# Hybrid decoder step: the products of a weight unit ordered by output tile, and in the FFN blocks in sixteen orders by turns

## The chip, the cores and the metric

The kernel runs on one core of one Trainium2 chip. The page of the profile names the core's engines: PE multiplies matrices (PEld is its loading of the stationary operand), DVE and ACT work elementwise, POOL does a little elementwise work and issues DMAs, SP issues DMAs. The metric is the device time of one execution in microseconds; of several executions the median counts.

## The reference, cut to what matters

One layer works on 256 prompt tokens and 8 × 4 sample tokens, 288 columns in all, with a model width of 2048 and an FFN width of 5632.

```
x = x + 0.5 * rmsnorm(swiglu(rmsnorm(x, g0), ffn1_w_in, ffn1_w_out), g1)
x = x + rmsnorm(hybrid_mixer(rmsnorm(x, g2), mix_w_in, ..., mix_w_out), g3)
x = x + 0.5 * rmsnorm(swiglu(rmsnorm(x, g4), ffn2_w_in, ffn2_w_out), g5)

swiglu(x):        gate, up = split(x @ w_in, 2);  (silu(gate) * up) @ w_out
hybrid_mixer(h):  proj = h @ w_in                 # q, k, v, gates of two groups of heads
                  two recurrences S_t = diag(a_t) S_{t-1} + k_t^T v_t, o_t = q_t S_t
                  merged @ w_out
```

The outputs are y for the prompt and for the sample, and the recurrent states of both. All of it is float32.

## The kernel before, in words

The tokens are the columns of every product: a tile of activations is 128 features by 288 tokens. For accuracy each float32 operand is kept as a high and a low part, and a product of two operands is made as three matmuls into one PSUM tile. `mm3` records them, always in this order; this document calls them A, B and C.

- A (line 596): high weights by high activations
- B (line 597): high weights by low activations
- C (line 598): low weights by high activations

Weights come from memory in *units* of 128 × 1024 numbers, two activation tiles' worth (k = 2u and 2u + 1, called the two *halves* of the unit) by 512 output columns. `Weights.load` issues the DMA on SP, and `Weights.pieces` makes the high part on ACT (line 100) and the low part on DVE (line 101). Up to three raw units and four split ones are held; each engine's order is the order in which the program records the work, and `W.ahead` records further splits after each unit.

`block` (line 587) makes one block of 512 output columns: four PSUM tiles f = 0 to 3 of 128 columns, from all units. A block of the FFNs' input side (`gate` and `up`, eleven of each in each FFN) and each block of the mixer has 16 activation tiles, so eight units, of 4 × 2 × 3 = 24 matmuls each, 192 in all. A block of the FFNs' output side (`out`) has two units (48 matmuls), the last four in each FFN have four. In all units of a block but the last, the order before is by activation tile: for each half, for each f, the three matmuls A, B, C. The last unit, the *tail*, goes by output tile: for each f, both halves, A, B, C of each. After each f of the tail that tile is evacuated from PSUM (`evac`): in a gate block by DVE at line 676. There are five PSUM tiles for blocks, so a block's tiles f = 1, 2, 3 take the places of the block before's f = 0, 1, 2.

An FFN goes through chunks c = 0 to 10: gate c, up c, then the four out blocks of chunk c − 1. In the first blocks after a norm (`gate1_0`, `qk0`, `gate2_0`) the activation tiles become ready one after another while the block runs. In the mixer, `tick` records pieces of the recurrences between products, small matmuls among them, after each activation tile. In the mixer's last gate block, `tick_last` records the splits of the merged outputs (`split_y`), which overwrite the activation tiles that this block reads.

Of the kernel before, what the change touches and what calls it, by code (L numbers as in the profile page):

```python
# [16 lines left out]
P = 128  # L17
TP = 256
TS = 32
T = TP + TS  # L20
# [3 lines left out]
KT = D // P  # L24
# [14 lines left out]
class Weights:  # L39
# [91 lines left out]
def trunk_kernel(ctx, tc, x_prompt, x_sample, state_gla, state_hgrn, norm_gains, f1_in, f1_out, f2_in, f2_out,  # L131
# [3 lines left out]
    V, S, G, PE = nc.vector, nc.scalar, nc.gpsimd, nc.tensor  # L135
# [107 lines left out]
    FIRST = 2  # L243
# [339 lines left out]


    product = [None]

    def block(name, nk, rhs, evac, width=512, tick=None, tail=1, hold=False, most=99, fill=None, late=0):

        nf, per = width // P, 1024 // width
        nu = nk // per  # L590
        ps = [mmtile(f"{name}_{f}") for f in range(nf)]
        ws = [W.next() for _ in range(EARLY // per)] if fill else []

        def mm3(dst, w, f, k, parts, start, stop):
            a, c = k % per, slice(f * P, f * P + P)
            yield lambda: PE.matmul(dst, w[0][:, a, c], parts[0], start=start, stop=False)  # L596
            yield lambda: PE.matmul(dst, w[0][:, a, c], parts[1], start=False, stop=False)  # L597
            yield lambda: PE.matmul(dst, w[1][:, a, c], parts[0], start=False, stop=stop)  # L598

        def mm(w, f, k):  # L600
            if not fill or f or k >= EARLY:
                for ready in mm3(ps[f][:, 0:T], w, f, k, rhs(k), k == 0, k == nk - 1):
                    product[0] = ready().ins

        if fill:
            fill.products(lambda dst, k, parts, stop: mm3(dst, ws[k // per], 0, k, parts, k == 0, stop), ps[0][:, 0:T])
        for u in range(nu - tail):
            w = ws.pop(0) if ws else W.next()
            for k in range(u * per, (u + 1) * per):
                if fill and k < UPDATED:  # L610
# [38 lines left out]
    def ffn(tag, gcol, gnext, pn, before, fill=None):  # L649
# [3 lines left out]
        with ExitStack() as pools:  # L653
# [3 lines left out]
            def do_in(c):  # L657
                hh = fp.tile([P, 4, T], F32R, name=f"hh{tag}_{c}", tag="hh")
                hl = fp.tile([P, 4, T], F32R, name=f"hl{tag}_{c}", tag="hl")
                hid[c] = (hh, hl)  # L660
                gs = []

                def gate(g):
                    def run():
                        V.tensor_tensor(g, g, rt, op=ALU.mult)
                        act(g, g, AF.Silu)
                    return run

                def ev_gate(f, ps):
                    g = fp.tile([P, T], F32, name="g", tag="g", bufs=6)  # L670
                    gs.append(g)
                    if c == 0:
                        W.behind = S.activation(g, ps, AF.Copy).ins
                        pn.late.append(gate(g))
                    else:
                        V.tensor_tensor(g, ps, rt, op=ALU.mult)
                        act(g, g, AF.Silu)

                def ev_up(f, ps):
                    u = fp.tile([P, T], F32, name="u", tag="u", bufs=3)  # L680
                    V.tensor_tensor(u, ps, rt, op=ALU.mult)  # L681
                    V.tensor_tensor(u, u, gs[f], op=ALU.mult)
                    S.activation(hh[:, f, :], u, AF.Copy)
                    V.tensor_tensor(hl[:, f, :], u, hh[:, f, :].bitcast(F32), op=ALU.subtract)

                if c == 0:
                    block(f"gate{tag}_0", KT, xrhs, ev_gate, tick=pn.tick0, most=1 if final else 0, fill=fill,
                          late=0 if final else FIRST)
                    before.close()
                    if not final:  # L690
                        border.append(Border(mixer_start, hg1, gnext, 5, 2))
                else:
                    block(f"gate{tag}_{c}", KT, xrhs, ev_gate)
                if final and c == 0:
                    last_pool()
                block(f"up{tag}_{c}", KT, xrhs, ev_up, tick=pn.tick1 if c == 0 else None)

            lasts, zs, blocks = [], [], []

# [167 lines left out]
    def mixer(pn, border):  # L867
        with ExitStack() as mx:
# [667 lines left out]
            for g in range(2):  # L1536
                d = group_tiles(f"g{g}")
                block(f"qk{g}", KT, xrhs, ev_gla(d, g == 0), tick=tick if g else pn.tick0, most=99 if g else 1,
                      fill=None if g else border.fill)
                if g == 0:  # L1540
                    scan_pool()
                if g == 0:
# [55 lines left out]
            def split_y(t):  # L1598
                S.activation(xh[t], y[t], AF.Copy)
                V.tensor_tensor(xl[t], y[t], xh[t].bitcast(F32), op=ALU.subtract)  # L1600
# [6 lines left out]
                    tick(k)  # L1607

            def tick_last(k):
                if k < 12:  # L1610
                    split_y(k)

            for n in range(4):
                block(f"gate{n}", KT, xrhs, ev_gate(n), tick=(tick, tick, tick_silu, tick_last)[n])
# [79 lines left out]
```

## Time and profile before

| | us |
|---|---|
| three runs | 2226.94, 2227.61, 2229.22 |
| median | 2227.61 |
| profiled execution | 2226.28 |
| its span, first to last instruction | 2224.5 |
| PE busy | 2212.8 |
| DVE busy | 1386.7 |
| ACT busy | 1020.1 |
| POOL busy | 180.2 |

Engines work at the same time, so the busy times don't add up to the span. PE's matmuls overlap each other in the records (a row of 0.29 us is followed by the next after some 0.13 us); what a matmul costs in a row of them is therefore read from the distance of starts, not from the duration.

### The profile page before, as it was taken

How to read it: one execution, taken by the hardware profiler on the slowest of the kernel's cores; microseconds unless marked ns; L12 is line 12 of the kernel's file. 1: busy time of each engine (PE TensorE's matmuls, PEld its weight loads, DVE VectorE, ACT ScalarE, POOL GpSimd, SP SyncE). 2: the span in 40 equal slices, each digit the busy share in tenths (PEclk: the TensorE clock that was granted, in tenths of full speed). 3: DMA queues.
4: the chain of work that ended last, by engine and by line, in shares of the span. 5: the costliest groups of instructions: out<-in, count | busy, mean ns of one | idle time of the engine just before them, and what ended most of it. 6: DMA issues, size and time to landing. Idle time of an engine off the chain costs nothing. (4 is left out here: it accounts for less than half of the span.)

```text
span 2224.5 us, 43196 instructions
## 1 busy us (share of the span) xinstructions
PE 2212.8 (99%) x17820; PEld 2197.9 (99%) x17820; DVE 1386.7 (62%) x2254; ACT 1020.1 (46%) x1535; POOL 180.2 (8%) x327
## 2 busy tenths in 40 slices
PE   9999999999999999999999999999999999999998
PEld 9999999999999999999999999999999999999998
DVE  7645546554555568888888755844555466556646
ACT  6453333333334345655676654543333333333344
POOL 2000000000000001233210000000000020122005
PEclk9999999999999999999999999999999999999999
DMA  7555555555555554667566564555555565566555
GB/s 224 173 166 167 170 167 166 170 165 168 171 164 181 177 165 139 193 204 214 171 188 179 174 185 133 171 168 165 170 167 165 170 176 168 179 178 176 171 162 159
DMA packets 227334, 384.87 MB, mean 173 GB/s; under 512 B 21362, under 2 KB 60864, under 8 KB 227136
## 3 DMA queue, kind: packets, MB, share of 16 engines
q1 hardware_dynamic: 213776, 364.89, 54.8%
q0 software_dynamic: 10992, 16.77, 2.9%
q8 instruction: 140, 2.29, 0.4%
q10 hardware_dynamic: 2368, 0.44, 0.1%
q14 instruction: 58, 0.48, 0.1%
HBM read 363.75 MB, written 11.80 MB: 169 GB/s over the span
## 5 line engine op out<-in xcount | busy, mean ns | idle before, releaser
L101 DVE TENSOR_TENSOR wh<-raw,wh 128x1024 fp32r<-128x1024 f32 (+1 forms) x676 | 821.8, 1217 | 619.0 <-ACT wh L100 617.5
L100 ACT ACTIVATE wh<-raw 128x1024 fp32r<-128x1024 f32 (+1 forms) x676 | 711.0, 1053 | 961.0 <-PE gate L598 301.8
L596 PE MATMUL gate<-xh,wh 128*128 128x288 f32 x1660 | 485.5, 294 | 0.0
L598 PE MATMUL gate<-xh,wh 128*128 128x288 f32 x1660 | 484.8, 293 | 0.0
L597 PE MATMUL gate<-xl,wh 128*128 128x288 f32 x1660 | 484.7, 294 | 0.0
L597 PE MATMUL out<-hl,wh 128*128 128x288 f32 x1408 | 416.2, 296 | 0.0
L597 PE MATMUL up<-xl,wh 128*128 128x288 f32 x1408 | 413.9, 294 | 0.0
L598 PE MATMUL up<-xh,wh 128*128 128x288 f32 x1408 | 412.8, 293 | 0.0
L598 PE MATMUL out<-hh,wh 128*128 128x288 f32 x1408 | 412.1, 293 | 0.0
L596 PE MATMUL up<-xh,wh 128*128 128x288 f32 x1408 | 411.8, 293 | 0.0
L596 PE MATMUL out<-hh,wh 128*128 128x288 f32 x1408 | 411.5, 292 | 0.0
L596 PEld LDWEIGHTS gate<-xh,wh 128*128 128x128 f32 x1660 | 311.2, 188 | 0.8 <-DVE u L681 0.4
L598 PEld LDWEIGHTS gate<-xh,wh 128*128 128x128 f32 x1660 | 311.1, 188 | 0.2 <-DVE wh L101 0.2
L597 PEld LDWEIGHTS gate<-xl,wh 128*128 128x128 f32 x1660 | 310.5, 188 | 0.5
L596 PEld LDWEIGHTS out<-hh,wh 128*128 128x128 f32 x1408 | 264.9, 188 | 0.0
L596 PEld LDWEIGHTS up<-xh,wh 128*128 128x128 f32 x1408 | 264.4, 188 | 0.0
L597 PEld LDWEIGHTS out<-hl,wh 128*128 128x128 f32 x1408 | 264.3, 188 | 0.0
L598 PEld LDWEIGHTS out<-hh,wh 128*128 128x128 f32 x1408 | 264.3, 188 | 0.0
L597 PEld LDWEIGHTS up<-xl,wh 128*128 128x128 f32 x1408 | 264.2, 188 | 0.0
L598 PEld LDWEIGHTS up<-xh,wh 128*128 128x128 f32 x1408 | 264.2, 188 | 0.0
L770 DVE TENSOR_TENSOR y<-out,y 128x288 f32<-128x288 f32 x287 | 120.7, 452 | 85.2 <-PE out L598 84.1
L727 POOL DMA_DIRECT2D xT<-b x64 | 37.2, 588 | 764.8 <-PE gate L598 571.8
(410 smaller groups left out, 2550.3 us busy)
## 6 DMA issues: line engine op xcount, KB each, us to landing
raw<-in_ffn_w_in_dram SPq DMA_DIRECT2D x350, 512.0 KB, 3.6
raw<-in_ffn_w_out_dram SPq DMA_DIRECT2D x176, 512.0 KB, 3.6
raw<-in_mix_w_in_dram SPq DMA_DIRECT2D x64, 512.0 KB, 4.1
raw<-in_mix_w_in_dram SPq DMA_DIRECT2D x96, 256.0 KB, 3.2
raw<-in_mix_w_out_dram SPq DMA_DIRECT2D x32, 512.0 KB, 3.8
out_dram<-s POOLq DMA_DIRECT2D x32, 256.0 KB, 2.9
s<-in_state_gla_dram SPq DMA_DIRECT2D x16, 256.0 KB, 4.9
s<-in_state_hgrn_dram SPq DMA_DIRECT2D x16, 256.0 KB, 5.2
```

The source lines that it names most:

```text
L100: i1 = self.nc.scalar.activation(h[:, a, c], raw[:, a, c], AF.Copy).ins
L101: i2 = self.nc.vector.tensor_tensor(l[:, a, c], raw[:, a, c], h[:, a, c].bitcast(F32), op=ALU.subtract).ins
L596: yield lambda: PE.matmul(dst, w[0][:, a, c], parts[0], start=start, stop=False)
L597: yield lambda: PE.matmul(dst, w[0][:, a, c], parts[1], start=False, stop=False)
L598: yield lambda: PE.matmul(dst, w[1][:, a, c], parts[0], start=False, stop=stop)
L727: queues[n % len(queues)].dma_start(dst[q * TS:(q + 1) * TS, 4 * g:4 * g + 4, :, cols].rearrange("p k t c -> p (k t) c"), b32[rows, q])
L770: V.tensor_tensor(y[k], ps, y[k], op=ALU.add)
```

## The change

Three things change, all in the order in which `block` records its matmuls. No matmul, transfer or elementwise instruction is added or removed.

1. By default a unit's matmuls now go as the tail's do, by output tile: for each f, both halves, A, B, C of each. `tick` is called after f = 1 and after f = 3, so as often as before and after as many matmuls. This holds for all out blocks, for `up1_0` and `up2_0`, for all blocks of the mixer but `qk0`, and for the `mo` blocks (the mixer's output projection).
2. `gate1_0`, `gate2_0` and `qk0` keep the old order (`byk=True`).
3. The 40 other gate and up blocks (c = 1 to 10 in both FFNs) take, for all units but the tail, one of sixteen orders from the table `ways`: gate takes number (20·tag + 2c) mod 16 and up the next, where tag is 1 or 2.

With `split_y` called two activation tiles later, no tile is overwritten that a later f of the same unit still reads.

The sixteen orders differ in what changes from one matmul to the next. By how often two successive matmuls belong to different halves of the unit, and so to different activation tiles k, they fall into four groups:

| Half changes | Orders | Blocks |
|---|---|---|
| after every 3 matmuls, as in the tail | 0, 1, 3, 6, 14, 15 | 13 |
| after every 6 | 12, 13 | 6 |
| after every 12, as in the order before | 8, 9, 10 | 9 |
| after every one (2, 5, 11) or after 4 of 6 (4, 7) | 2, 4, 5, 7, 11 | 12 |

Order 15 also takes the output tiles from f = 3 down to 0. The diff, with two of the sixteen rows for f, half a and product j in full:

```diff
     product = [None]
-
-    def block(name, nk, rhs, evac, width=512, tick=None, tail=1, hold=False, most=99, fill=None, late=0):
+    by = lambda fs, kj: [(f, a, j) for f in fs for a, j in kj]
+    A, B, C = 0, 1, 2
+    ways = [
+        by(range(4), [(0, A), (0, B), (0, C), (1, A), (1, B), (1, C)]),
...
+        by(range(4), [(0, A), (1, A), (0, B), (1, B), (0, C), (1, C)]),
...
+        [(f, a, j) for a in range(2) for f in range(4) for j in range(3)],
...
+        [(f, a, j) for f in range(3, -1, -1) for a in range(2) for j in range(3)],
+    ]
+
+    def block(name, nk, rhs, evac, width=512, tick=None, tail=1, hold=False, most=99, fill=None, late=0, byk=False, way=None):
...
         for u in range(nu - tail):
             w = ws.pop(0) if ws else W.next()
-            for k in range(u * per, (u + 1) * per):
+            if way is not None:
+                for f, a, j in ways[way]:
+                    k = u * per + a
+                    q, r = ((0, 0), (0, 1), (1, 0))[j]
+                    begin = u == 0 and (f, a, j) == next(e for e in ways[way] if e[0] == f)
+                    product[0] = PE.matmul(ps[f][:, 0:T], w[q][:, a, f * P:f * P + P], rhs(k)[r],
+                                           start=begin, stop=False).ins
+            elif not byk:
+                for f in range(nf):
+                    for k in range(u * per, (u + 1) * per):
+                        mm(w, f, k)
+                    if tick is not None and f % 2:
+                        tick(u * per + f // 2)
+            for k in range(u * per, (u + 1) * per) if byk else ():
...
-                    block(f"gate{tag}_{c}", KT, xrhs, ev_gate)
+                    block(f"gate{tag}_{c}", KT, xrhs, ev_gate, way=(20 * tag + 2 * c) % 16)
...
-                block(f"up{tag}_{c}", KT, xrhs, ev_up, tick=pn.tick1 if c == 0 else None)
+                block(f"up{tag}_{c}", KT, xrhs, ev_up, tick=pn.tick1 if c == 0 else None,
+                      way=(20 * tag + 2 * c + 1) % 16 if c else None)
...
             def tick_last(k):
-                if k < 12:
-                    split_y(k)
+                if 2 <= k < 14:
+                    split_y(k - 2)
```

What stands in PE's row at three places, in the names that the program gives: `mo2_1` is tile f = 1 of the third `mo` block, `xh1` and `xl1` are the high and the low part of activation tile 1, `wh` is a split unit. Lines 596 to 598 of the kernel before are lines 616 to 618 now; the sixteen orders are recorded at line 634.

PE at the start of block `mo2` (an out block reads likewise, with the FFN's inner activations in place of `xh` and `xl`), before:

```order
L596 MATMUL mo2_0_15486<-xh0_114,wh392_15320 128x288
L597 MATMUL mo2_0_15486<-xl0_130,wh392_15320 128x288
L598 MATMUL mo2_0_15486<-xh0_114,wh392_15320 128x288
L596 MATMUL mo2_1_15487<-xh0_114,wh392_15320 128x288
L597 MATMUL mo2_1_15487<-xl0_130,wh392_15320 128x288
L598 MATMUL mo2_1_15487<-xh0_114,wh392_15320 128x288
L596 MATMUL mo2_2_15488<-xh0_114,wh392_15320 128x288
```

PE at the same place now:

```order
L616 MATMUL mo2_0_15486<-xh0_114,wh392_15320 128x288
L617 MATMUL mo2_0_15486<-xl0_130,wh392_15320 128x288
L618 MATMUL mo2_0_15486<-xh0_114,wh392_15320 128x288
L616 MATMUL mo2_0_15486<-xh1_115,wh392_15320 128x288
L617 MATMUL mo2_0_15486<-xl1_131,wh392_15320 128x288
L618 MATMUL mo2_0_15486<-xh1_115,wh392_15320 128x288
L616 MATMUL mo2_1_15487<-xh0_114,wh392_15320 128x288
```

Six matmuls now go to one output tile in succession, three of each half, where three did.

PE in the first unit of `gate1_7`, which takes order 2, before:

```order
L598 MATMUL gate1_7_0_5579<-xh0_114,wh160_5473 128x288
L596 MATMUL gate1_7_1_5580<-xh0_114,wh160_5473 128x288
L597 MATMUL gate1_7_1_5580<-xl0_130,wh160_5473 128x288
L598 MATMUL gate1_7_1_5580<-xh0_114,wh160_5473 128x288
L596 MATMUL gate1_7_2_5581<-xh0_114,wh160_5473 128x288
```

PE in the same unit now, from its third matmul on:

```order
L634 MATMUL gate1_7_0_5579<-xl0_130,wh160_5473 128x288
L634 MATMUL gate1_7_0_5579<-xl1_131,wh160_5473 128x288
L634 MATMUL gate1_7_0_5579<-xh0_114,wh160_5473 128x288
L634 MATMUL gate1_7_0_5579<-xh1_115,wh160_5473 128x288
L634 MATMUL gate1_7_1_5580<-xh0_114,wh160_5473 128x288
```

Here the half changes with every matmul.

PE at the border of `gate1_5` and `up1_5`, which takes order 15, before:

```order
L596 MATMUL gate1_5_3_4042<-xh15_129,wh119_4154 128x288
L597 MATMUL gate1_5_3_4042<-xl15_145,wh119_4154 128x288
L598 MATMUL gate1_5_3_4042<-xh15_129,wh119_4154 128x288
L596 MATMUL up1_5_0_4287<-xh0_114,wh120_4183 128x288
L597 MATMUL up1_5_0_4287<-xl0_130,wh120_4183 128x288
```

PE at the same border now:

```order
L616 MATMUL gate1_5_3_4042<-xh15_129,wh119_4154 128x288
L617 MATMUL gate1_5_3_4042<-xl15_145,wh119_4154 128x288
L618 MATMUL gate1_5_3_4042<-xh15_129,wh119_4154 128x288
L634 MATMUL up1_5_3_4290<-xh0_114,wh120_4183 128x288
L634 MATMUL up1_5_3_4290<-xl0_130,wh120_4183 128x288
```

Tile f = 3, which takes the PSUM place of `gate1_5`'s f = 2, is now written first where it was written tenth. On DVE, ACT, POOL and SP the order of the instructions is the one before, but for the mixer's last gate block, where each weight split now stands one `split_y` earlier among the splits.

More of the change, by code (lines that the diff above doesn't have):

```diff
@@ L585, in trunk_kernel @@
     product = [None]
-    def block(name, nk, rhs, evac, width=512, tick=None, tail=1, hold=False, most=99, fill=None, late=0):
+    by = lambda fs, kj: [(f, a, j) for f in fs for a, j in kj]
+    A, B, C = 0, 1, 2
+    ways = [
+        by(range(4), [(0, A), (0, B), (0, C), (1, A), (1, B), (1, C)]),
+        by(range(4), [(0, A), (0, C), (0, B), (1, A), (1, C), (1, B)]),
+        by(range(4), [(0, A), (1, A), (0, B), (1, B), (0, C), (1, C)]),
+        by(range(4), [(0, A), (0, B), (0, C), (1, C), (1, B), (1, A)]),
+        by(range(4), [(0, B), (0, A), (1, A), (1, B), (0, C), (1, C)]),
+        by(range(4), [(0, A), (1, A), (0, C), (1, C), (0, B), (1, B)]),
+        by(range(4), [(0, C), (0, A), (0, B), (1, B), (1, A), (1, C)]),
+        by(range(4), [(0, A), (0, B), (1, A), (1, B), (0, C), (1, C)]),
+        [(f, a, j) for a in range(2) for f in range(4) for j in range(3)],
+        [(f, a, j) for a in range(2) for j in range(3) for f in range(4)],
+        [(f, a, j) for a in range(2) for f, j in [(f, j) for f in range(4) for j in (A, C)] + [(f, B) for f in range(4)]],
+        [(f, a, j) for j in range(3) for f in range(4) for a in range(2)],
+        [(f, a, j) for g in range(2) for a in range(2) for j in range(3) for f in (2 * g, 2 * g + 1)],
+        [(f, a if f % 2 else 1 - a, j) for f in range(4) for a in range(2) for j in range(3)],
+        [(f, a, j if f % 2 else 2 - j) for f in range(4) for a in range(2) for j in range(3)],
+        [(f, a, j) for f in range(3, -1, -1) for a in range(2) for j in range(3)],
+    ]
+    def block(name, nk, rhs, evac, width=512, tick=None, tail=1, hold=False, most=99, fill=None, late=0, byk=False, way=None):
         nf, per = width // P, 1024 // width
@@ L687, in do_in @@
                     block(f"gate{tag}_0", KT, xrhs, ev_gate, tick=pn.tick0, most=1 if final else 0, fill=fill,
-                          late=0 if final else FIRST)
+                          late=0 if final else FIRST, byk=True)
                     before.close()
@@ L1538, in mixer @@
                 block(f"qk{g}", KT, xrhs, ev_gla(d, g == 0), tick=tick if g else pn.tick0, most=99 if g else 1,
-                      fill=None if g else border.fill)
+                      fill=None if g else border.fill, byk=not g)
                 if g == 0:
```

## The prediction

> **What bounds the kernel now.** I read the page's busy times first, then PE's waits, then the busy time of single blocks, and last the matmuls in order of time.
>
> ```profile
> span 2224.5 us, 43196 instructions
> PE 2212.8 (99%) x17820; PEld 2197.9 (99%) x17820; DVE 1386.7 (62%) x2254; ACT 1020.1 (46%) x1535; POOL 180.2 (8%) x327
> ...
> PEclk9999999999999999999999999999999999999999
> ```
>
> PE is busy for 99% of the span at the full granted clock. The list of waits (who waited for whom, total, times, longest) has little for PE, and its longest single wait is at the start:
>
> ```profile
> PE warm L311 <- POOL onesD L233: 1.1, 1, 1.1
> PE sc L1063 <- ACT R L1053: 0.7, 2, 0.4
> ```
>
> The weight splits run ahead of PE. ACT waits for PE before it may split another unit, since the buffers are full:
>
> ```profile
> ACT wh L100 <- PE gate L598: 301.8, 150, 2.3
> ```
>
> So the time is the number of matmuls by the distance at which they follow each other, and nothing that another engine does is on the path but in a few places of the mixer. Four stretches follow: the blocks gate1_5, up1_5, the four out blocks after them, and the mixer from qk0 to gate1. The columns are length, then PE, PEld, DVE, ACT, POOL busy with their instructions, and the granted clock.
>
> ```profile
> 363.46:388.67 25.21, 25.21 (x194) 25.21 (x193) 11.36 (x13) 9.07 (x10) 0.00 (x0) 1.00 0.56 168
> 388.67:413.89 25.22, 25.22 (x195) 25.22 (x194) 11.37 (x13) 9.55 (x12) 0.00 (x0) 1.00 0.54 167
> 413.89:439.06 25.17, 25.17 (x195) 25.17 (x193) 18.66 (x33) 9.89 (x12) 0.00 (x0) 1.00 0.57 168
> 842.30:1222.40 380.10, 378.52 (x3875) 366.16 (x3875) 323.92 (x717) 235.63 (x511) 86.42 (x154) 1.00 0.64 184
> ```
>
> Each of the first three holds 192 matmuls (the counts include neighbours): 25.21 / 192 = 131.30 ns each in gate1_5, 25.17 / 192 = 131.09 in the out blocks. The out blocks have half their units in the tail's order, gate1_5 an eighth. Is the tail's order quicker, then? The matmuls of gate1_5 in order of time (start, duration): its first; a pair ahead of the tail, and the tail's first; the tail's tenth; the first of up1_5.
>
> ```profile
> 363.46 0.29 PE L596 MATMUL gate<-xh,wh 128*128 128x288 f32 x1
> ...
> 385.41 0.29 PE L598 MATMUL gate<-xh,wh 128*128 128x288 f32 x1
> 385.53 0.29 PE L596 MATMUL gate<-xh,wh 128*128 128x288 f32 x1
> ...
> 386.72 0.29 PE L596 MATMUL gate<-xh,wh 128*128 128x288 f32 x1
> ...
> 388.67 0.29 PE L596 MATMUL up<-xh,wh 128*128 128x288 f32 x1
> ```
>
> Seven units of the old order: (385.53 − 363.46) / 168 = **131.37** ns a matmul. The tail: 3.14 / 24 = **130.83**. Within the tail the first nine take 1.19 / 9 = 132.2, the last fifteen 1.95 / 15 = **130.0**. The same instructions on the same operands thus follow each other 1.4 ns sooner, once the tail's order has run for nine matmuls. In a profile of one execution, rows to 0.01 us bound the 130.0 to ±0.7; the two block means agree with the pair 131.37 and 130.83, since half of each gives 131.10 against 131.09.
>
> **The change part by part.** Nothing is added or removed, so each term is a count of matmuls by a difference of distances.
>
> *Out blocks.* 80 blocks, 4224 matmuls, all in the tail's order now, unit after unit. From 131.09 to 130.0: 4224 × 1.09 = 4.6 us. If each unit has to find its rhythm anew, a unit costs 130.83 and only the 94 units that were in the old order gain: 2256 × 0.54 = 1.2 us. I take 4.6: the first nine of the tail follow another order, while a unit in the tail's order would follow one like itself.
>
> *Eight whole blocks that run undisturbed*: up1_0, up2_0, the mixer's gate2 and gate3, four mo blocks. From 131.30 to 130.0, 192 × 1.30 = 0.25 us each, 2.0 in all; 0.7 if each unit begins anew.
>
> *Eleven mixer blocks with the recurrences' small matmuls between* (qk1, v0, v1, hi, hfq, gate0, gate1). Their 2112 matmuls lie in the last stretch above, 380.10 us for twelve blocks with qk0, where 2304 matmuls at 131.37 are 302.7. The small ones break the rhythm every dozen or two. Between 0 and 11 × 0.25 = 2.75; half, 1.4. The small matmuls stand after as many large ones as before, so what they wait for has as long to come.
>
> *FFN blocks with orders that change half every 3* (13 blocks): as the undisturbed ones, 13 × 0.25 = 3.25 us, lower end 13 × 168 × 0.54 = 1.2. *Every 12* (9 blocks): the old rate, 0. *Every 6* (6 blocks): between these, 6 × 0.125 = 0.75, ends 0 and 1.5.
>
> *Half changes after nearly each matmul* (12 blocks, 12 × 168 = 2016 matmuls). The nearest rows are the ends of qk0 and gate2_0, where B, C of one half and A, B, C of the other follow for each f; first and last of 18 matmuls:
>
> ```profile
> 870.71 0.29 PE L596 MATMUL qk<-xh,wh 128*128 128x288 f32 x1
> ...
> 872.95 0.30 PE L598 MATMUL qk<-xh,wh 128*128 128x288 f32 x1
> ...
> 1402.84 0.29 PE L596 MATMUL gate<-xh,wh 128*128 128x288 f32 x1
> ...
> 1405.06 0.29 PE L598 MATMUL gate<-xh,wh 128*128 128x288 f32 x1
> ```
>
> One order, two rates: 2.24 / 17 = 131.8 and 2.22 / 17 = 130.6. Their mean is 131.2, 0.17 under the old: 2016 × 0.17 = 0.3 us. Ends: 130.0 gives 2.8 gained, 131.8 gives 0.9 lost.
>
> *Waits for PSUM.* Order 15 writes f = 3 first, in the place of the block before's f = 2. DVE evacuates gate1_5's f = 1, 2, 3 in one go, behind a weight split:
>
> ```profile
> 386.90 1.22 DVE L101 TENSOR_TENSOR wh<-raw,wh 128x1024 fp32r<-128x1024 f32 x1
> 388.04 1.29 DVE L676 TENSOR_TENSOR g<-gate,rt 128x288 f32<-128x288 f32 x3
> ```
>
> f = 2 is out at 388.04 + 2 × 0.43 = 388.90, and PE would want its place at 388.67: 0.25 us lost, in two blocks, 0.5. Before, f = 3 came tenth, at 389.85, and this was covered by 0.95 us. Order 9 writes it fourth, at 389.06, still covered by 0.16; all others later.
>
> *The mixer's last gate block.* Each split_y stands one weight split later on ACT and DVE; tiles 12 to 15 come after the block as before, and mo0 begins with tile 0. Covered by the whole block; nothing.
>
> Sum: 4.6 + 2.0 + 1.4 + 3.25 + 0 + 0.75 + 0.3 − 0.5 = 11.8 us off the profiled execution's 2226.28, so 2214.5. The median of the runs lies 1.33 above that execution (2227.61): **2215.8 us**, 0.5% faster. With the ends of the disturbed, every-6 and every-1 groups it spans 2211 to 2219 (16.4 and 8.5 us off).
>
> **The rivals.**
> - *The rhythm starts anew with each unit.* For it: the tail's first nine are slow, and a unit's border changes the weight buffer. Against it: the tail's quick part crosses from one f to the next freely, and up1_5 and the block after it begin without a gap. Then 1.2 + 0.7 + 1.2 + 0.3 (mixer) − 0.5 = 2.9: 2224.7.
> - *The order doesn't matter*, and the tail is quicker for another reason, say that fewer splits write beside it. The windows' DVE share speaks against that: 18.66 us in the out blocks against 11.36, and those are not slower. Then 2227.6. The Trainium skill (SBUF — State Buffer, Who interferes with whom) gives PE two independent read ports, one for the moving operand and one for the weights, and lets only the port pair of DVE and GpSimd contend. By that rule order is free; the 131.37 and 130.0 of one block do not agree with it.
> - *Half changes at every matmul are quick.* Matmuls can start 0.12 us apart (385.41 and 385.53). If order 2 and its kin reach 0.125, the twelve blocks gain 2016 × 6.4 = 12.9 in place of 0.3: 2203. Against it: in the steady tail a short distance is followed by long ones, and qk0's end has no gain. The Trainium skill (TensorE: Matmul & The Clock Gate, Back-to-back issue gap) puts a lone matmul of 288 columns at 288/2.4 + 2.5 = 122.5 ns; at that estimate these blocks would gain 17.9 us. No stretch of this trace runs so.
> - *Half changes at every matmul are dear*: each moves both the weights' and the activations' address, in twelve gate and up blocks. Everything else gains 11.5 us, so they decide the sign from 131.37 + 11.5 / 2.016 = 137.1 ns on; at 140 the result is 2227.6 − 11.5 + 17.4 = 2233.5. Against it: qk0's 131.8.
>
> **How the numbers follow.** My forecast 0.62, anew with each unit 0.13, order doesn't matter 0.09, quick 0.09, dear 0.07. Quick and a part of dear are left out of the range: 2206 to 2226.5; the likeliest alone has 2211 to 2219. About 0.2% (4.5 us) can be told from no change here. Faster: 0.62 + 0.09 and a third of "anew", 0.75; within 0.2%: the rest of "anew" and "doesn't matter", 0.18; slower 0.07.
>
> **What would show it.** In the matmuls in order of time, the out blocks' 192 (four blocks) should last 24.96 to 25.0 us against 25.17, and gate blocks with order 0, 1, 3, 6 or 14 the same against 25.21; orders 8 to 10 should stay at 25.2. Blocks with orders 2, 5 and 11 tell the two last rivals apart: under 24.5 or over 26. The two blocks with order 15 should show one PE gap of about 0.25 us at their start. If out blocks stay above 25.1, the rhythm doesn't carry from unit to unit, and the prediction is wrong at its largest term.

## The result and the profile after

| | before | after |
|---|---|---|
| median of the runs, us | 2227.61 (2226.94 to 2229.22) | 2219.35 (2218.68 to 2219.71) |
| profiled execution, us | 2226.28 | 2219.33 |
| its span, us | 2224.5 | 2217.5 |

The changed kernel takes 0.9962 of the time before, with a 95% interval of 0.995 to 0.9974. It is 8.3 us faster, where 11.8 were forecast. The page of the profile shows the same picture as before: PE busy for 99% of the span, the other engines doing what they did.

```profile
span 2217.5 us, 43190 instructions
PE 2205.0 (99%) x17820; PEld 2190.1 (99%) x17820; DVE 1386.2 (63%) x2254; ACT 1020.0 (46%) x1535; POOL 179.6 (8%) x327
```

So the question is again how far apart the matmuls start. These are the busy times of single stretches of the trace after, in the columns used before: gate1_5 (order 14), up1_5 (order 15), the four out blocks behind them, gate1_7 (order 2), gate1_4 (order 12), gate1_2 (order 8), and the mixer from qk0 to gate1.

```profile
362.99:387.95 24.96, 24.96 (x194) 24.96 (x193) 11.36 (x13) 9.07 (x10) 0.00 (x0) 1.00 0.58 169
387.95:412.91 24.96, 24.96 (x194) 24.96 (x193) 11.36 (x13) 9.55 (x12) 0.00 (x0) 1.00 0.54 169
412.91:437.87 24.96, 24.96 (x195) 24.96 (x193) 18.65 (x33) 9.89 (x12) 0.00 (x0) 1.00 0.55 169
512.75:538.12 25.37, 25.37 (x195) 25.37 (x194) 11.37 (x13) 9.09 (x10) 0.00 (x0) 1.00 0.57 167
287.20:312.62 25.42, 25.42 (x195) 25.42 (x193) 11.36 (x13) 9.07 (x10) 0.00 (x0) 1.00 0.59 166
136.28:161.49 25.21, 25.21 (x194) 25.21 (x193) 10.72 (x11) 9.37 (x11) 0.00 (x0) 1.00 0.57 167
839.31:1218.71 379.40, 377.62 (x3876) 365.22 (x3875) 323.75 (x717) 235.63 (x511) 86.15 (x154) 1.00 0.65 184
```

A block of 192 matmuls in 24.96 us has them 130.0 ns apart. The first three stretches, whose halves change every 3 matmuls, run so from end to end, across the borders of units, blocks and PSUM tiles; before, the same places took 25.21, 25.22 and 25.17. Order 8, where the half changes every 12, takes 25.21 as before (131.3 ns). But order 2, with the half changing at every matmul, takes 25.37 (132.1) and order 12, every 6, takes 25.42 (132.4): both are *slower* than the order they replaced.

Adding up the lengths of all blocks in the two traces, from the first matmul of a block to the next block's (or, where small matmuls stand between, the distances behind the block's own matmuls):

| group | forecast gain, us | gain in the traces, us |
|---|---|---|
| 80 out blocks | 4.6 | 4.7 |
| eight undisturbed blocks | 2.0 | 1.9 |
| eleven mixer blocks | 1.4 | 0.8 |
| FFN orders, half every 3 (13 blocks) | 3.25 | 3.25 |
| FFN orders, half every 12 (9) | 0 | −0.2 |
| FFN orders, half every 6 (6) | 0.75 | −1.2 |
| FFN orders, half nearly every matmul (12) | 0.3 | −1.7 |
| order 15's wait for PSUM | −0.5 | 0 (in the 3.25) |
| all else | 0 | −0.6 |
| sum | 11.8 | 7.0, the spans' difference |

The forty FFN blocks with the table's orders thus come out at 3.25 − 0.2 − 1.2 − 1.7 = +0.15 us, and the gain is that of the other blocks, which took one plain order. The 0.2 lost in the every-12 group is one block, gate2_1 (order 10): its steady units have 132.5, those of the other eight 131.4.

### The profile page after: what moved, and what is told of

Same layout as the page of the kernel before. It is cut to its first block, busy times and chain, and to the rows that moved or that the text cites. A ratio compares the mean times of both kernels' runs of the same rounds, so it can differ in the third digit from the quotient of the medians.

```text
span 2217.5 us, 43190 instructions
## 1 busy us (share of the span) xinstructions
PE 2205.0 (99%) x17820; PEld 2190.1 (99%) x17820; DVE 1386.2 (63%) x2254; ACT 1020.0 (46%) x1535; POOL 179.6 (8%) x327
## 5 line engine op out<-in xcount | busy, mean ns | idle before, releaser
L634 PE MATMUL gate<-xh,wh 128*128 128x288 f32 x2240 | 407.4, 294 | 0.1
L634 PE MATMUL up<-xh,wh 128*128 128x288 f32 x2240 | 404.7, 294 | 0.0
L634 PEld LDWEIGHTS up<-xh,wh 128*128 128x128 f32 x2240 | 341.0, 188 | 0.0
L634 PEld LDWEIGHTS gate<-xh,wh 128*128 128x128 f32 x2240 | 339.6, 188 | 0.5 <-DVE u L714 0.5
L634 PE MATMUL up<-xl,wh 128*128 128x288 f32 x1120 | 274.5, 295 | 0.0
L634 PE MATMUL gate<-xl,wh 128*128 128x288 f32 x1120 | 273.7, 294 | 0.0
L634 PEld LDWEIGHTS up<-xl,wh 128*128 128x128 f32 x1120 | 191.9, 188 | 0.0
L634 PEld LDWEIGHTS gate<-xl,wh 128*128 128x128 f32 x1120 | 191.2, 188 | 0.0
L616 PE MATMUL gate<-xh,wh 128*128 128x288 f32 x540 | 157.3, 295 | 0.0
L617 PE MATMUL gate<-xl,wh 128*128 128x288 f32 x540 | 156.6, 297 | 0.0
L618 PE MATMUL gate<-xh,wh 128*128 128x288 f32 x540 | 156.4, 293 | 0.0
L616 PEld LDWEIGHTS gate<-xh,wh 128*128 128x128 f32 x540 | 101.3, 189 | 0.4
L618 PEld LDWEIGHTS gate<-xh,wh 128*128 128x128 f32 x540 | 101.0, 188 | 0.2 <-DVE wh L101 0.2
```

Of the source, the lines that this page charges most:

```text
L634: product[0] = PE.matmul(ps[f][:, 0:T], w[q][:, a, f * P:f * P + P], rhs(k)[r], start=begin, stop=False).ins
```

## The experiments

Each kernel is compared with runs of the kernel before on the same chip: 2227.84 us (13 runs) for the first four kernels below, 2227.74 (7) for the two that have pairs and a second changed block, 2227.36 (14) for the other four. "Tail" is the order of the tail, by output tile; "old" the order before, by activation tile. Distances are means over the starts of a block's matmuls in order of time; where a block begins and ends in another rhythm, its units but the tail are given.

### Without the table

The tail's order in all forty blocks, nothing else differs from the changed kernel:

```diff
-                    block(f"gate{tag}_{c}", KT, xrhs, ev_gate, way=(20 * tag + 2 * c) % 16)
+                    block(f"gate{tag}_{c}", KT, xrhs, ev_gate)
...
-                block(f"up{tag}_{c}", KT, xrhs, ev_up, tick=pn.tick1 if c == 0 else None,
-                      way=(20 * tag + 2 * c + 1) % 16 if c else None)
+                block(f"up{tag}_{c}", KT, xrhs, ev_up, tick=pn.tick1 if c == 0 else None)
```

> The changed kernel without the table: the forty gate and up blocks too take the tail's order (order 0) in every unit. If the rate of an undisturbed block is a property of its order alone, each of the 27 blocks that now run at 131.3 to 132.4 ns a matmul comes to 130.0: 9 blocks x 0.25 us + 6 x 0.45 + 12 x 0.40 = 9.8 us off the changed kernel, 2209.5. If the 130.0 of the blocks beside them needed a change of orders around them, less.

Measured: 2209.25, 2209.62, 2209.67, 2210.3, 2221.42, 2222.7, 2222.85 and 2236.8 us; median 2215.86, ratio 0.996 (0.9933 to 0.9988), though one ratio says little of times that stand in steps. Four of eight executions are where they were expected, the others some 12 and once 27 us above. The profiled one was among the four (2209.62), with 130.0 ns in nearly every block. That one program on one chip has several times, so regularly spaced, was not in the theory. If one whole FFN ran at 132.2 instead of 130.0, that would be 20 gate and up blocks and out blocks worth 11 more, 31 × 192 × 2.2 ns = 13 us; both would be 26. The later runs take this up.

And the old order in all forty blocks:

```diff
-                    block(f"gate{tag}_{c}", KT, xrhs, ev_gate, way=(20 * tag + 2 * c) % 16)
+                    block(f"gate{tag}_{c}", KT, xrhs, ev_gate, byk=True)
...
-                      way=(20 * tag + 2 * c + 1) % 16 if c else None)
+                      byk=c > 0)
```

> The changed kernel with the forty gate and up blocks in the order before (half by half). Their rows in the changed kernel say that the sixteen orders together gain almost nothing: 13 blocks gain 0.25 us each, 12 lose some 0.14, 6 lose 0.20, 9 are unchanged, 0.35 us in all. So 2219.7, the whole gain of the change being in the out, mo and mixer blocks. If the orders carried more than that (by their effect on neighbours), over 2222.

Measured: 2220.29 (2219.65 to 2220.87), ratio 0.9966 (0.9954 to 0.9978). gate1_5 and the four out blocks of chunk 4 in its trace:

```profile
362.98:388.20 25.22, 25.22 (x195) 25.22 (x194) 11.37 (x13) 9.08 (x10) 0.00 (x0) 1.00 0.58 168
413.41:438.38 24.97, 24.97 (x195) 24.97 (x194) 18.65 (x33) 9.88 (x12) 0.00 (x0) 1.00 0.56 169
```

The old order takes 25.22, the out blocks 24.97 as in the changed kernel. So the rest of the change is worth 7.6 us by itself (2227.84 − 2220.29). The changed kernel is 0.9 lower (2219.35), which the two intervals do not tell apart; by its blocks the table is worth the 0.15 above.

### What sets the distance: made-up sequences

Each of the forty blocks gets a sequence of its own for all units but the tail, in place of its products, so the FFNs' results are left out. A row names PSUM tile, columns of the weights, half of the weight unit, activation tile, and which parts are taken; some of the forty:

```diff
+    def abc(seq):
+        return [(f, f, aw, kd, q, r) for f, aw, kd in seq for q, r in ((0, 0), (0, 1), (1, 0))]
...
+    def only(seq):
+        return [(f, fw, aw, kd, 0, 0) for f, fw, aw, kd in seq]
...
+    def runs(n, aw, kd):
+        return only([(0, 0, aw[i // n % 2], kd[i // n % 2]) for i in range(24)])
...
+        abc([(f, a, a) for f in F4 for a in range(2)]),
...
+        abc([(f, a, 0) for f in F4 for a in range(2)]),
+        abc([(f, 0, a) for f in F4 for a in range(2)]),
+        abc([(f, 0, 0) for f in F4 for a in range(2)]),
...
+        runs(2, (0, 1), (0, 1)),
+        runs(3, (0, 1), (0, 1)),
...
+        abc([(f, a, (0, 3)[a]) for f in F4 for a in range(2)]),
+        abc([(f, a, (0, 4)[a]) for f in F4 for a in range(2)]),
...
+        runs(24, (1, 1), (0, 0)),
+        runs(24, (0, 0), (1, 1)),
```

> The forty gate and up blocks repeat forty made-up rows of matmuls in place of their products in seven of eight units (the tail stays): the FFNs' results are left out. It asks what of an order makes its rate. Theory 1, addresses: the rate depends on where the activations that stream and the weights that load lie to each other, and a half change matters because weights and activations move in two steps. Then switching between activation tiles whose addresses agree modulo 512 B (0 and 4) is as no switch, switching the weights' half alone or the activations' alone gives other rates than both together, and constant rows at another relative place differ from each other. Theory 2, rhythm: only the number of matmuls between changes counts, whatever changes: 3 gives 130.0, 12 gives 131.4, 6 gives 132.6, 1 gives 132.3, for addresses that agree too. Theory 3, PSUM: six successive matmuls into one tile are what makes the tail quick; then three in one tile with the half changing every 3 gives 131.4 or more.

The second kernel has the same rows, and no pad between the two halves of a weight unit. With the pad of 32 columns the second half lies 4224 B behind the first, without it 4096 B; neighbouring activation tiles are 1152 B apart. 4224 and 1152 both leave 128 when divided by 256, and 4096 leaves 0. In the built programs all weight units and activation tiles begin at the same remainders of 256 with and without the pad, so the second halves alone are moved.

```diff
-HALF = 1024 + 32
+HALF = 1024
```

> The same forty rows with the pad of 32 columns between the two halves of a split weight unit taken away, so that the second half's weights lie 128 B nearer: the FFNs' results are left out. Theory 1: rows with half changes move, the tail's order away from 130.0 by 0.5 ns or more, and constant rows of the first half stay. Theories 2 and 3: every row as with the pad, within 0.1 ns.

Measured, one time each: 2222.97 us with the pad and 2239.49 without. Nine blocks of the first kernel (up1_2, gate1_3, up1_3, up1_7, up2_1, gate2_2, up2_3, gate2_4, up2_4), whose sequences the table below names:

```profile
161.03:186.39 25.36, 25.36 (x195) 25.36 (x194) 11.38 (x13) 9.56 (x12) 0.00 (x0) 1.00 0.53 167
211.35:236.69 25.34, 25.34 (x194) 25.34 (x193) 11.36 (x13) 9.08 (x10) 0.00 (x0) 1.00 0.58 167
236.69:261.95 25.26, 25.26 (x194) 25.26 (x193) 11.37 (x13) 9.56 (x12) 0.00 (x0) 1.00 0.55 167
539.57:564.95 25.38, 25.38 (x194) 25.38 (x193) 11.36 (x13) 9.58 (x12) 0.00 (x0) 1.00 0.53 166
1452.79:1477.75 24.96, 24.96 (x194) 24.96 (x193) 11.34 (x13) 9.55 (x12) 0.00 (x0) 1.00 0.54 169
1502.71:1528.07 25.36, 25.36 (x194) 25.36 (x193) 10.74 (x11) 9.39 (x11) 0.00 (x0) 1.00 0.58 167
1602.95:1628.49 25.54, 25.54 (x194) 25.54 (x193) 11.37 (x13) 9.55 (x12) 0.00 (x0) 1.00 0.53 166
1653.45:1678.98 25.53, 25.53 (x194) 25.53 (x193) 11.36 (x13) 9.06 (x10) 0.00 (x0) 1.00 0.56 165
1678.98:1704.24 25.26, 25.26 (x194) 25.26 (x193) 11.37 (x13) 9.56 (x12) 0.00 (x0) 1.00 0.53 167
```

Five of the second (gate1_2, up1_2, gate1_7, up2_3, gate2_4):

```profile
138.04:163.43 25.39, 25.39 (x194) 25.39 (x193) 10.75 (x11) 9.43 (x11) 0.00 (x0) 1.00 0.58 166
163.43:188.72 25.29, 25.29 (x194) 25.29 (x193) 11.35 (x13) 9.58 (x12) 0.00 (x0) 1.00 0.53 167
518.28:543.86 25.58, 25.58 (x195) 25.58 (x194) 11.36 (x13) 9.11 (x10) 0.00 (x0) 1.00 0.57 165
1615.86:1641.15 25.29, 25.29 (x194) 25.29 (x193) 11.35 (x13) 9.58 (x12) 0.00 (x0) 1.00 0.54 167
1666.54:1692.11 25.57, 25.57 (x194) 25.57 (x193) 11.36 (x13) 9.12 (x10) 0.00 (x0) 1.00 0.58 166
```

The mean distance from the third to the seventh unit of the block (ns):

| sequence | with pad | without |
|---|---|---|
| no change of half at all (up1_3) | 131.67 | 131.67 |
| the same, weights' second half (up2_3) | 133.32 | 131.67 |
| the same, second activation tile (gate2_4) | 133.33 | 133.33 |
| the same, third activation tile (up2_4) | 131.67 | 131.67 |
| weights' half changes every 3, one activation tile (up1_2) | 132.22 | 131.67 |
| activations change every 3, one weights' half (gate1_3) | 132.22 | 132.22 |
| both, and the output tile every 3 instead of every 6 (gate1_2) | 130.0 | 132.22 |
| both, with activation tile k + 3 for k + 1 (up2_1) | 130.0 | 132.22 |
| both, with k + 4 for k + 1 (gate2_2) | 132.22 | 131.67 |
| both, every 2 (gate1_7) | 131.67 | 133.33 |
| both, every 3, on one output tile, right behind that (up1_7) | 132.22 | 132.22 |

Three things follow. *One*: with constant operands the rate has two values, 131.67 and 133.3, and in these rows it goes by how the weights' and the activations' addresses lie to each other modulo 256 B: moving one of them by an odd number of 128 B changes the rate, moving the activations by two tiles (2304 B, nine times 256) does not, nor the weights' half without the pad. No row moves both and stays there, but the old order does so for twelve matmuls at a time: in the kernel before, the distances inside either half of a unit have the same mean, 131.8; without the pad, in the kernel below, those inside the second half alternate between 130.0 and 136.7, 133.3 on average. *Two*: with both changing every 3 the rate falls to 130.0, but only if each change moves *both* by an odd number of 128 B. The pad does that for the weights, and without it the whole second kernel finds no 130.0 anywhere: its out blocks are all at 132.2. *Three*: which output tile is written, or how often it changes, has no effect that these rows show: the 130.0 of gate1_2 has another order of tiles than the tail's, and turning through PSUM tiles or weights' columns with constant halves stays at 131.67. The theory of the PSUM tiles fell with that.

By the Trainium skill (SBUF — State Buffer, Who interferes with whom) PE reads moving operand and weights by two independent ports. These rows do not agree with that in one respect: the distance of two matmuls depends on how the two addresses lie to each other.

The last row of the table is odd: the same succession of halves as in the tail, and 132.22 instead of 130.0; and the out blocks behind it, in the tail's own order, stayed at 132.2 as well, while they were at 130.0 behind most others.

That the pad alone matters so much was then tried on the kernel before:

> The kernel before without the pad of 32 columns between the halves of a split unit. The probe without the pad had the old order at 132.8 and the tail behind it at 132.1, against 131.4 and 130.8 with it. If addresses modulo 256 B set the rate, the kernel before becomes slower by some 1.3 ns x 14,000 undisturbed matmuls = 18 us: 2246. If the probe's difference came from its made-up rows, it stays at 2228.

Measured: 2244.87 (2244.58 to 2246.0), ratio 1.0079 (1.0064 to 1.0094), with `HALF = 1024` in the kernel before and nothing else. gate1_5 and the out blocks of chunk 4:

```profile
366.72:392.19 25.47, 25.47 (x195) 25.47 (x193) 11.37 (x13) 9.12 (x10) 0.00 (x0) 1.00 0.57 166
417.65:443.04 25.39, 25.39 (x194) 25.39 (x193) 18.66 (x33) 9.87 (x12) 0.00 (x0) 1.00 0.56 167
```

25.47 and 25.39 against 25.21 and 25.17 with the pad: the address of the second half is worth 17.5 us here, twice what the change gained.

### Two rhythms of one order

The theory now: the tail's order has two steady rhythms, 130.0 and 132.2, and a block hands its rhythm to the next. The old order, which had led, with the pad, to blocks at 130.0 behind it wherever it stood so far, should lead back to the first. So one block in each FFN gets the old order again (and the mixer's gate2), all others the tail's:

```diff
-                    block(f"gate{tag}_{c}", KT, xrhs, ev_gate, way=(20 * tag + 2 * c) % 16)
+                    block(f"gate{tag}_{c}", KT, xrhs, ev_gate, byk=c == 1)
...
-                block(f"gate{n}", KT, xrhs, ev_gate(n), tick=(tick, tick, tick_silu, tick_last)[n])
+                block(f"gate{n}", KT, xrhs, ev_gate(n), tick=(tick, tick, tick_silu, tick_last)[n], byk=n == 2)
```

> The kernel of e1 (tail order everywhere), but the first chunk's gate block in each FFN and the mixer's gate2 in the order before, half by half. The theory now: an order has more than one rhythm that keeps itself up, the tail's order 130.0 and 132.2 ns a matmul, and what ran before decides which; the old order leads into the quick one, whatever came before it. Then the executions of this kernel agree, where those of e1 lay at 2209.3 to 2210.3, 2221.4 to 2222.9 and 2236.8: 2209.5 + 3 x 0.25 = 2210.3, all within 2 us. If e1's scatter has another cause (the chip, DMA), it stays: some executions 10 us or more above the fastest.

Measured: 2210.27 (2210.12 to 2211.29), five runs, ratio 0.9924 (0.9911 to 0.9936). None of the five shows the steps of the kernel without the table, and this is the best kernel of the study. In its trace up2_0 ends at 132.21, and behind gate2_1 in the old order all is at 130.0. That alone does not show that the old order led there: in the trace of the kernel without the table, too, up2_0 ends at 132.21 and gate2_1, in the tail's order, goes on at 130.0. In both, PE waits near gate2_1's start; more on this wait below.

The reverse: in that kernel, one single block (gate1_2) whose half changes every 2, all products kept:

```diff
+    ways = [by_halves([2] * 12)]
...
-                    block(f"gate{tag}_{c}", KT, xrhs, ev_gate, byk=c == 1)
+                    block(f"gate{tag}_{c}", KT, xrhs, ev_gate, byk=c == 1, way=0 if (tag, c) == (1, 2) else None)
```

> The kernel of e5 with one block more changed: gate1_2 takes an order in which the half changes after every 2 matmuls (the probe had 131.7 there, and the tail behind it at 132.2). If a rhythm is handed on, every undisturbed block of FFN 1 behind it (16 gate and up blocks and 40 out blocks of a quarter's length, 27 x 192 matmuls with the out blocks of chunks 9 and 10 counted double) runs at 132.2 though not a byte of its code differs from e5: 27 x 0.43 = 11.5 us, 2222; FFN 2, behind its own old-order block, is at 130.0. If a block's rate is its own, 0.3 us: 2210.6.

Measured: 2221.85 (2220.11 to 2223.8), seven runs, ratio 0.9976 (0.9965 to 0.9986): 24 rearranged matmuls a unit in one block cost 11.6 us. gate1_2, up1_2, gate1_5, out1_8_1 and gate1_10 of this kernel:

```profile
136.75:162.04 25.29, 25.29 (x194) 25.29 (x193) 10.76 (x11) 9.41 (x11) 0.00 (x0) 1.00 0.58 167
162.04:187.43 25.39, 25.39 (x194) 25.39 (x193) 11.36 (x13) 9.59 (x12) 0.00 (x0) 1.00 0.54 167
365.14:390.52 25.38, 25.38 (x194) 25.38 (x193) 11.36 (x13) 9.12 (x10) 0.00 (x0) 1.00 0.58 167
726.90:733.17 6.27, 6.27 (x51) 6.27 (x49) 5.00 (x10) 2.12 (x2) 0.00 (x0) 1.00 0.81 240
745.65:770.61 24.96, 24.96 (x195) 24.96 (x193) 11.36 (x13) 9.07 (x10) 0.00 (x0) 1.00 0.59 169
```

up1_2 and gate1_5 of the kernel without pairs:

```profile
161.52:186.48 24.96, 24.96 (x194) 24.96 (x193) 11.36 (x13) 9.55 (x12) 0.00 (x0) 1.00 0.55 169
361.20:386.16 24.96, 24.96 (x194) 24.96 (x193) 11.36 (x13) 9.08 (x10) 0.00 (x0) 1.00 0.58 169
```

gate1_5 is the same code in both, with busy times of DVE and ACT that agree to 0.04 us, 200 us behind the pairs, and takes 25.38 in one and 24.96 in the other. The distances of starts in one of its units repeat as 126, 133, 131 ns (390 for three) in the quicker and as 131, 132, 134, 130, 133, 133, 131, 133, 133 in the other. All blocks from up1_2 to out1_8_0 ran at 132.2, and then out1_8_1 found back in the middle. The trace records no wait there. But in the traces of the kernel with the old order in all forty blocks and of the next kernel below PE waits at the seventh matmul of out1_8_1 for DVE's evacuation of out1_8_0: the two distances there add up to 780 and 527 ns in place of some 260. Here that evacuation was done 0.16 us before the matmul. Whether so near a miss turned the rhythm is not shown.

To see whether an order can lead back on purpose, the same kernel with pairs, and two chunks later gate1_4 in the old order, or in order 2 of the table, which changes half at every matmul:

```diff
-                    block(f"gate{tag}_{c}", KT, xrhs, ev_gate, byk=c == 1, way=0 if (tag, c) == (1, 2) else None)
+                    block(f"gate{tag}_{c}", KT, xrhs, ev_gate, byk=c == 1 or (tag, c) == (1, 4), way=0 if (tag, c) == (1, 2) else None)
```

> The kernel with one block of pairs (gate1_2), and two chunks later the old order in gate1_4. If a block hands its rhythm on, and the old order leads out of the slow one: gate1_2 at 131.7, up1_2, the out blocks of chunk 1, gate1_3, up1_3 and the out blocks of chunk 2 at 132.2, gate1_4 near 131.4 to 131.6 with its tail near 130.8, everything from up1_4 on at 130.0. Six slow blocks cost 0.33 + 5 x 0.43 = 2.5 us and gate1_4 0.3: 2213 us (2211 to 2215). If the slow rhythm ends only by itself at some later point, the old order does nothing for it: out blocks of chunk 3 and later at 132.2, and 2220 to 2224 us as with the pairs alone.

```diff
-    ways = [by_halves([2] * 12)]
+    ways = [by_halves([2] * 12), [(f, a, j) for f in range(4) for j in range(3) for a in range(2)]]
...
-                    block(f"gate{tag}_{c}", KT, xrhs, ev_gate, byk=c == 1, way=0 if (tag, c) == (1, 2) else None)
+                    block(f"gate{tag}_{c}", KT, xrhs, ev_gate, byk=c == 1, way={(1, 2): 0, (1, 4): 1}.get((tag, c)))
```

> The same with order 5's kin in gate1_4, halves changing after every product (A, A, B, B, C, C of the two halves for each output tile), as twelve blocks of the change nearly have it. If such a block of the change also leads out of the slow rhythm: gate1_4 at 132.2, its tail between 130.8 and 131.2, all from up1_4 on at 130.0, 2213 us (2211 to 2215); that would say why the change, whose table has such blocks throughout, was never seen slow. If it hands the slow rhythm on: its tail at 132.2, out blocks of chunk 3 at 132.2, 2220 to 2224 us; then the change was quick only because nothing in it led into the slow rhythm.

Measured: 2213.41 (2212.67 to 2214.55), ratio 0.9932 (0.9915 to 0.9949), and 2213.26 (2212.95 to 2214.0), ratio 0.9933 (0.9918 to 0.9948); both the first theory's 2213. The out blocks of chunk 2, gate1_4 and up1_4, with the old order:

```profile
263.62:289.00 25.38, 25.38 (x194) 25.38 (x193) 18.64 (x33) 9.85 (x12) 0.00 (x0) 1.00 0.55 167
289.00:314.23 25.23, 25.23 (x195) 25.23 (x193) 11.32 (x13) 9.07 (x10) 0.00 (x0) 1.00 0.59 167
314.23:339.19 24.96, 24.96 (x195) 24.96 (x193) 11.36 (x13) 9.55 (x12) 0.00 (x0) 1.00 0.54 170
```

and with order 2:

```profile
262.65:288.04 25.39, 25.39 (x195) 25.39 (x193) 18.64 (x33) 9.85 (x12) 0.00 (x0) 1.00 0.56 167
288.04:313.40 25.36, 25.36 (x194) 25.36 (x193) 11.32 (x13) 9.09 (x10) 0.00 (x0) 1.00 0.57 166
313.40:338.36 24.96, 24.96 (x194) 24.96 (x193) 11.35 (x13) 9.55 (x12) 0.00 (x0) 1.00 0.55 170
```

In both, 132.2 ahead of gate1_4 and 130.0 behind it, with no wait of PE in between. The second block is itself no quicker than what came before, and still leads to 130.0. This would explain why the changed kernel's four executions held to 2218.7 to 2219.7 where the kernel without the table scattered: in its table no more than two chunks in succession (those with orders 14, 15, 0 and 1) are without an order that changes half in another way than every 3, and all its out blocks are at 130.0. Of its orders, the old one (8) and order 2 were tried from the 132.2 side, the others not.

### No better order was found

Forty complete orders, which differ only in the lengths of the runs of one half:

```diff
+    ways = [by_halves(lengths) for lengths in (
+        [3, 3, 3, 3, 3, 3, 3, 3],
+        [4, 4, 4, 4, 4, 4],
...
+        [6, 6, 6, 6],
+        [5, 5, 7, 7],
```

> The forty gate and up blocks take forty orders with all their products, which differ only in the runs of equal halves (3 3 3 3 ..., 4 4 ..., 12 12, 11 11 1 1, and irregular ones). If the halves' sequence alone makes the rate, the ones that were seen come back: threes at 130.0 or 132.2, fours 130.8, twos 131.7, sixes 132.6 to 132.8, twelves 131.4. No sequence below 130.0 is expected: that is the least that any steady stretch has shown. If one is below 129.5, a better order exists than the tail's.

One time, 2223.58. None was below 130.0. In steady units: fours 130.83, mixed lengths 131.1 to 132.5, twelves 131.4, twos 131.67, sixes 132.8. The threes stood at 132.22 here, and the fours behind them led back. Four of the mixed orders left the blocks behind them at 132.2, as the twos did. up1_1 (fours) and gate1_3 (sixes):

```profile
86.40:111.53 25.13, 25.13 (x195) 25.13 (x193) 11.32 (x13) 9.56 (x12) 0.00 (x0) 1.00 0.55 168
211.96:237.38 25.42, 25.42 (x195) 25.42 (x194) 11.37 (x13) 9.08 (x10) 0.00 (x0) 1.00 0.58 166
```

The threes are the tail's order, in gate1_1, and the block ahead of them had not handed them the slow rhythm: up1_0's last unit, gate1_1, and PE's wait at gate1_1's seventh matmul for DVE to evacuate up1_0.

```profile
57.69:60.81 3.12, 3.12 (x27) 3.12 (x25) 3.12 (x8) 3.11 (x8) 0.00 (x0) 1.00 0.60 168
60.81:86.40 25.59, 25.59 (x195) 25.41 (x193) 17.18 (x28) 11.01 (x16) 0.00 (x0) 1.00 0.63 170
PEld gate L663 <- DVE u L743: 0.2, 1, 0.2
```

The same in the profiled execution of the kernel without the table, whose gate1_1 has the same matmuls in the same order:

```profile
57.53:60.65 3.12, 3.12 (x27) 3.12 (x26) 3.12 (x8) 3.11 (x8) 0.00 (x0) 1.00 0.59 170
60.65:85.85 25.20, 25.20 (x195) 25.02 (x194) 17.14 (x28) 10.99 (x16) 0.00 (x0) 1.00 0.63 173
PEld gate L616 <- DVE u L714: 0.2, 1, 0.2
```

Both come in at 130.0 (24 matmuls in 3.12 us) and wait about as long (the two distances at the wait add up to 478 and 483 ns); behind it the one goes on at 132.22 and the other at 130.0. So a wait of PE can change the rhythm as well, either way. The old order in gate1_1 comes out of this wait in two ways too: its steady units have 132.5 in the kernel with one block in the old order, 131.4 in that with the pairs, and both lead to 130.0. Such a wait, of 0.1 to 0.3 us, stands near the start of gate1_1 in every trace and near that of gate2_1 in all but one, each ahead of most of an FFN.

## Why the prediction was right, and where not

2219.35 us lies in the range of 2206 to 2226.5 and on the side forecast with 0.75, but just outside the 2211 to 2219 that the likeliest case had for itself.

- *Out blocks*: right. 24.96 for four of them against 25.17, and the rhythm goes through from unit to unit. That refutes the rival by which it starts anew with each unit (2224.7). The reading of the one tail, nine matmuls at 132.2 and fifteen at 130.0, was a reading of a rhythm being found, as taken.
- *Eight undisturbed blocks and the orders that change every 3*: right, 1.9 for 2.0 and 3.25 for 3.25. What the prediction did not see is that the tail's order can also settle at 132.2. Had that happened in these blocks, as it seems to have done in half of the executions without the table, these two terms and the first would have had the opposite sign. Nothing in the prediction excluded it, so that they came out at all was in part luck.
- *The order doesn't matter* (2227.6): refuted by the same rows.
- *Half changes every 6*: this step failed, +0.75 forecast as the middle between every 3 and every 12, −1.2 measured (25.42 a block against 25.21). The rate is not monotone in the length of the runs: 130.0 at 3, 130.8 at 4, 132.8 at 6, 131.4 at 12. The ends 0 and 1.5 did not hold it either, since both came from the interpolation.
- *Half changes after nearly each matmul*: this step failed, +0.3 forecast with ends −0.9 and 2.8, −1.7 measured. It was priced by the mean of two stretches of 18 matmuls, 131.8 and 130.6. Steady, the order runs at 132.2 (25.37 a block). That one order had shown two rates was the hint that so short a stretch tells what came before it as much as its own rate. Of the last two rivals, neither the quick (24.5 a block) nor the dear (26) is anywhere near.
- *Half changes every 12*: right but for the 0.2 us of gate2_1, which ran at 132.5, a second rhythm of such an order.
- *Disturbed mixer blocks*: right in sign, 0.8 for 1.4 by the blocks; the stretch from qk0 to gate1 fell from 380.10 to 379.40. Here the second rhythm did come up: v0's two long stretches between small matmuls run at 132.2 in the trace after, where they ran at 131.0 to 132.2 before, and v0 and v1 together lost 0.1 us.
- *Order 15's wait*: this step failed, 0.5 forecast, 0 measured. The rows at the border of gate1_5 and up1_5 after show starts 0.12 to 0.13 apart and no gap:

```profile
387.82 0.29 PE L618 MATMUL gate<-xh,wh 128*128 128x288 f32 x1
387.95 0.29 PE L634 MATMUL up<-xh,wh 128*128 128x288 f32 x1
388.07 0.30 PE L634 MATMUL up<-xl,wh 128*128 128x288 f32 x1
```

  The cause is in the program, not on the chip: a block's PSUM places are given out in the order in which its tiles are first written, not by f. In the built program gate1_5's four tiles lie in banks 1, 0, 4 and 3, and up1_5's f = 3 gets bank 2, the free one. The first tile written never waits, whichever it is, and what the part on the kernel before said of the places holds only for orders that begin with f = 0.

The two failed groups together missed by 1.95 + 2.0, some 4.0 us, the mixer by 0.6, work that was not in the sum by 0.6 and the every-12 group by 0.2; the wait that did not come gave 0.5 back. That is, to rounding, the 4.8 between 11.8 and 7.0.

## What to carry to other kernels

Where PE is busy throughout, the order of the matmuls and the addresses of their two operands count even if nothing waits (here 0.8% of the time each): look at the mean distance of starts in whole blocks and over units that repeat, not at 18 matmuls, before an order is priced. If an order has more than one steady rhythm, the best case of one profile is not its time: run it several times, and if the times stand in steps, put a block with an order that leads to the quicker rhythm ahead of each long stretch; here a kernel with three such blocks ran 2210 to 2211 us five times, where eight executions without them took 2209 to 2237. An alignment pad in a weight buffer should be tested by itself.

## What was not expected of the hardware

- Two matmuls of 288 columns start 131.67 or 133.3 ns apart with constant operands, and moving the weights or the activations by an odd number of 128 B turns one into the other. Moving both so, every three matmuls, gives 130.0, less than either, or in its second rhythm 132.2. What in the chip makes this was not found; the runs show only that PSUM tiles and columns of the weights have no part in it.
- The same code on the same data runs at 130.0 or 132.2 for hundreds of microseconds, by what ran before it or by how it came out of a wait of 0.2 us, and neither weight loads nor PSUM evacuation differ in the records. Pairs and some mixed lengths lead to 132.2; the old order, fours, and halves changing at every matmul lead to 130.0. Why the kernel with pairs once found back by itself (at out1_8_1) is open. Why the kernel without the table takes the one or the other from execution to execution is not shown either; the wait near the start of gate1_1 and of gate2_1, after which the same matmuls went either way, is a likely place. Its slower executions were not profiled: that they are FFNs at 132.2 rests on the sizes of the steps.
- In the kernel before, having the second half of a weight unit 128 B further on is worth 17.5 us in 2227.
